# Decode cache values: from weighted rows summed by a selector matmul to cache values as TensorE's stationary operand

## The chip, the cores and the metric

The kernel runs on one core of a Trainium2 chip. The metric is device time in microseconds, from the first to the last instruction and what the launch adds around it; lower is better. The kernel before was run three times: 1863.29, 1864.06 and 1867.74 us, a median of 1864.06 us. One further execution was profiled; it took 1859.84 us, and its span, from the first to the last instruction that the profiler recorded, is 1858.1 us. All times "at" which something happens count from the start of that span.

## The reference, cut to what matters

The model is one layer of a hybrid decoder. A prompt of 1024 positions and eight decode rows (one new position each, with caches of up to 2048 past positions) go through the same weights. The mixer has three patterns of dilated sliding-window attention (g = 0, 1, 2; 8 heads of 64) and a state-space branch. Two places of it are touched here.

The prompt's three patterns are merged position by position, weighted by their softmax denominators:

```python
def merge_patterns(outs, lses):
    alpha = jax.nn.softmax(jnp.stack(lses, axis=0), axis=0)
    o = sum(alpha[g][..., None] * outs[g] for g in range(N_PATTERNS))
    return o.reshape(o.shape[:-2] + (ATTN_OUT,))
```

The decode rows read, for each pattern, 128 cached keys and values (every first, fourth or sixteenth position) and the new one, and merge in the same way:

```python
    o = jnp.einsum('bthk,btkhd->bthd', p, sel[:, :, :, 1].astype(jnp.float32)) / den
```

So the decode output of row b and head h is a sum over three patterns and 128 positions of a softmax weight times a value row of 64 numbers, and a small term for the new position. In float32 this is 8 rows x 3 patterns x 128 positions x 512 values.

## The kernel before

Everything is float32. A projection is computed as three matmuls per tile, in float32r, on a high part and a low part: weights are loaded (`wr`, L149), rounded by ScalarE (`wh`, L164), and VectorE makes the rest (`wl = wr - wh`, L165). TensorE then runs `g += xh.wh + xh.wl + xl.wh` over eight k tiles of 128 (`unit`, L176): 24 matmuls of 344 columns make one tile of 128 outputs by a third of the 1032 columns (1024 prompt positions and 8 decode rows). `wr`, `wh` and `wl` have two buffers each.

The stage in question lies between the attention of the last pattern and the output projection, from about 870 to 1040 us. Its work, all in flight together:

- **z projection** (L870 to L893): for k = 0 to 7 a weight load, three tiles of 24 matmuls (L176), a copy out of PSUM by ScalarE (`zt`, L877), SiLU, and VectorE's product with the state-space result (`yg`, L886).
- **Weights of the prompt's merge** (L818 to L848): softmax statistics are loaded (`sn`), a chain of small VectorE steps makes `wo`, TensorE transposes it (`wtp`, L845), ScalarE copies it (`wts`, L847), and it is stored to DRAM as `w_d` (L848).
- **The prompt's merge** (L849 to L862): 16 pieces (four column quarters by four head pairs). A piece loads the three patterns' outputs (`nt`, 128x768, L853) and the weights, broadcast to 64 partitions twice (`wt`, two loads, L856). GpSimd multiplies them (L858), VectorE adds the three thirds (L859, L860), ScalarE rounds the sum (`ah`, L861), and VectorE makes the rest (`al`, L862). `nt` and `wt` have two buffers, so the load of piece i+2 waits for piece i: `nt` until its L862 is done, `wt` until its L858 is. Below the pieces are called a to p, in pairs; their `nt` tiles are numbered 8474, 8484, 8494 and so on to 8624.
- **Decode values** (L895 to L924): for each decode row b, three value tiles are loaded (`cvt`, 128 positions x 512, L904, six buffers). Each is multiplied by its softmax weights `dpt`, broadcast along 64 columns (L907; pattern 0 on VectorE, 1 and 2 on GpSimd), VectorE adds the three (L910, L911), and one float32 matmul with a selector column sums over the positions into row b of a PSUM tile (L912, 512 moving columns). At the end ScalarE copies the eight rows out (L915), four transposes turn them (L918), and VectorE adds the new positions' terms (`dat`, L919 to L921).
- **Output projection, state-space part** (L930 to L976): VectorE and ScalarE split `yg` into `sh` and `sl` (L935, L936), and TensorE starts the first two output tiles together, m = 0 and m = 1 (L957), with two weight loads of its own (`wl` of m = 0 and m = 1, made on VectorE like the z weights). The tiles m = 2 to 7 follow through `unit`.

Each engine runs its instructions in one fixed order, and so does SyncE, which issues all these DMAs. A scheduler builds the orders beforehand from priorities ("evac" first, then "w", "side", "late", and "main" for the big matmuls) and its own estimate of durations; on the chip an instruction that waits holds all that stand behind it in its engine's order. `behind(ins, prev)` only fixes an order on one engine: each decode row's first matmul stands behind a chosen tile of the z projection (`zlast[CACHE[b]]`). `sel`, the selector, is set up by two memsets (L897, L898).

Of the kernel before, what the change touches and what calls it, by code (L numbers as in the profile page):

```python
# [8 lines left out]
F32 = mybir.dt.float32  # L9
# [7 lines left out]
P = 128  # L17
# [33 lines left out]
def trunk(tc, a, o):  # L51
# [67 lines left out]
    def behind(ins, prev):  # L119

        tc.add_manual_dep(ins.ins, prev.ins.name,
                          mybir.DependencyInfo(mybir.DependencyClass.NoSync, mybir.DependencyReason.DATA),
                          reason="order")
# [694 lines left out]
    with prio("late"):  # L818
# [30 lines left out]
        for q in range(S // QT):  # L849
            for hp in range(HP):  # L850
                qs = slice(q * QT, (q + 1) * QT)
                nt = mgp.tile([P, NG, QT], F32, tag="nt", name="nt")
                nc.sync.dma_start(out=nt, in_=n_d[:, hp, :, qs].rearrange("g p t -> p g t"))  # L853
                wt = mgp.tile([P, NG, QT], F32, tag="wt", name="wt")
                for h in range(2):
                    nc.sync.dma_start(out=wt[h * 64:(h + 1) * 64],  # L856
                                      in_=w_d[:, 2 * hp + h, qs].unsqueeze(0).to_broadcast([64, NG, QT]))
                nc.gpsimd.tensor_tensor(out=nt, in0=nt, in1=wt, op=ALU.mult)  # L858
                nc.vector.tensor_tensor(out=nt[:, 0], in0=nt[:, 0], in1=nt[:, 1], op=ALU.add)  # L859
                nc.vector.tensor_tensor(out=nt[:, 0], in0=nt[:, 0], in1=nt[:, 2], op=ALU.add)  # L860
                nc.scalar.copy(ah[:, hp, qs], nt[:, 0])  # L861
                nc.vector.tensor_tensor(out=al[:, hp, qs], in0=nt[:, 0], in1=ah[:, hp, qs], op=ALU.subtract)  # L862
# [30 lines left out]
                    nc.gpsimd.tensor_tensor(out=acc, in0=acc, in1=zt, op=ALU.add)  # L893

    with prio("late"):  # L895
        sel = cap.tile([P, NB * NB], F32, name="sel")
        nc.vector.memset(sel, 0.0)  # L897
        nc.vector.memset(sel[:, 0:NB * NB:NB + 1], 1.0)  # L898
        ops = att_ps("nps")
        for b in range(NB):  # L900
            vts = []
            for g in range(NG):
                vt = cvp.tile([P, 512], F32, tag="cv", name="cvt")
                nc.sync.dma_start(out=vt, in_=a[f"cache{g}"][b].rearrange("(k r) c -> r k c", r=DIL[g])[0, :, 512:1024])  # L904
                pw = dpt[:, g].rearrange("p h (x b) -> p b x h", b=NB)[:, b].unsqueeze(3)
                v4 = vt.rearrange("p (x h d) -> p x h d", x=HP, h=2)
                (nc.gpsimd if g else nc.vector).tensor_tensor(out=v4, in0=v4, in1=pw.to_broadcast([P, HP, 2, 64]),  # L907
                                                              op=ALU.mult)
                vts.append(vt)
            nc.vector.tensor_tensor(out=vts[0], in0=vts[0], in1=vts[1], op=ALU.add)  # L910
            nc.vector.tensor_tensor(out=vts[0], in0=vts[0], in1=vts[2], op=ALU.add)  # L911
            behind(nc.tensor.matmul(ops[:NB], sel[:, b * NB:(b + 1) * NB], vts[0], start=(b == 0), stop=(b == NB - 1)),  # L912
                   zlast[CACHE[b]])
        osb = cvp.tile([NB, 512], F32, tag="cv", name="osb")
        nc.scalar.copy(osb, ops[:NB])  # L915
        otp = att_ps("nps")
        for hp in range(HP):
            nc.tensor.transpose(otp[:, hp * NB:(hp + 1) * NB], osb[:, hp * P:(hp + 1) * P], ident[:NB, :NB])  # L918
        nc.vector.tensor_tensor(out=dat, in0=otp[:, 0:HP * NB], in1=dnv[:, 0], op=ALU.add)  # L919
        for g in range(1, NG):  # L920
            nc.vector.tensor_tensor(out=dat, in0=dat, in1=dnv[:, g], op=ALU.add)  # L921
        dv = dat.rearrange("p (h b) -> p h b", h=HP)
# [584 lines left out]
```

## Time and profile before

| what | value |
|---|---|
| median of three runs | 1864.06 us (1863.29 to 1867.74) |
| profiled execution, its own time | 1859.84 us |
| its span | 1858.1 us |
| TensorE busy | 1773.7 us (95%) |
| VectorE busy | 1143.8 us (62%) |
| ScalarE busy | 782.1 us (42%) |
| GpSimd busy | 320.4 us (17%) |
| mean granted TensorE clock | 0.982 of 2.4 GHz |

TensorE is busy nearly everywhere, and the other engines far less. A busy share is an average over the whole program, so it doesn't tell what one stage is worth. For that one looks at a stretch of time: how long TensorE sat idle in it, at which clock it ran (a stretch shows 1.00 at 2.4 GHz, 0.50 at 1.2 GHz, and a mean of the two when both were granted), and what ended each idle time. "Chain of waits" means the chain of work that ended last, followed back from the end: at each step what released it.

### The profile page before, as it was taken

The page shows a single profiled execution, that of the slowest core. Times are in us where ns is not written, and L with a number is a line of the kernel's source. Part 1 is how long each engine was busy: PE and PEld are TensorE (multiplying, and loading weights), DVE is VectorE, ACT ScalarE, POOL GpSimd, SP SyncE. Part 2 cuts the span into 40 slices and gives each one's busy share as a digit, 9 for nine tenths or more (in the row PEclk, how much of TensorE's full clock was granted, in tenths as well). Part 3 has the DMA queues.
Part 4 walks back from the last instruction along what each step waited for, and adds up shares of the span by engine and source line. Part 5 has one row for each costly group of instructions (what it writes and reads, how often), then busy time and mean ns, then how long its engine had stood idle before and what let it go on. Part 6 is the DMA issues. An engine that isn't in the chain of part 4 may idle for free.

```text
span 1858.1 us, 30703 instructions
## 1 busy us (share of the span) xinstructions
PE 1773.7 (95%) x12189; PEld 1659.7 (89%) x12189; DVE 1143.8 (62%) x2236; ACT 782.1 (42%) x1441; POOL 320.4 (17%) x217
## 2 busy tenths in 40 slices
PE   8999999999998999999879999999999999999995
PEld 6999877888887888988768999999999999999995
DVE  6545666776765454446577599886666666423338
ACT  5533554465544555556343335532222222431133
POOL 0000244544224221123342300000000000000020
PEclk9999999999999999999989999999999999999998
DMA  4322344434334243346566345364454445876686
GB/s 156 136 99 79 96 127 124 130 121 125 105 103 156 90 141 108 117 158 230 154 172 187 108 155 178 111 211 166 172 175 159 177 152 204 335 276 205 207 316 206
DMA packets 135200, 298.61 MB, mean 161 GB/s; under 512 B 18432, under 2 KB 85600, under 8 KB 133648
## 3 DMA queue, kind: packets, MB, share of 16 engines
q1 hardware_dynamic: 135056, 296.64, 48.2%
q8 instruction: 96, 1.57, 0.4%
q14 instruction: 48, 0.39, 0.1%
HBM read 247.49 MB, written 137.10 MB: 207 GB/s over the span
## 4 chain that ended last, share of the span: by engine, by line
PE 37%; DVE 8%; DMA 4%; issue 1%; ACT 1%; POOL 0%; SPq 0%; DVEq 0%; POOLq 0%; ACTq 0%
PE fb L1230 21%; PE g L176 15%; DMA nt<-n_d 2%; PE pg L176 1%; PE pu L176 1%; DVE wl L165 1%; DVE xr L1056 1%; DVE sl L936 1%; DVE nacc L1013 1%; DMA hr<-hid_d 0%; DMA cvt<-in_cache 0%; DVE nt L859 0%; POOL nt L858 0%; DMA wr<-in_w_fin 0%; DVE fl L1071 0%
## 5 line engine op out<-in xcount | busy, mean ns | idle before, releaser
L176 PE MATMUL g<-xh,wh 128*128 128x344 f32 x1344 | 445.0, 331 | 4.4 <-ACT rw L589 3.7
L176 PE MATMUL g<-xh,wl 128*128 128x344 f32 x1344 | 438.9, 327 | 7.2 <-DVE wl L165 7.2
L176 PE MATMUL g<-xl,wh 128*128 128x344 f32 x1344 | 440.6, 328 | 1.5 <-DVE xl L234 1.5
L176 PEld LDWEIGHTS g<-xh,wh 128*128 128x128 f32 x1344 | 256.5, 191 | 17.8 <-issue 8.4
L176 PEld LDWEIGHTS g<-xh,wl 128*128 128x128 f32 x1344 | 257.0, 191 | 15.0 <-DVE wl L165 8.0
L176 PEld LDWEIGHTS g<-xl,wh 128*128 128x128 f32 x1344 | 256.9, 191 | 7.8 <-issue 4.9
L1230 PE MATMUL fb<-fh,wsl 128*128 128x258 f32 x1216 | 222.3, 282 | 0.0
L1230 PEld LDWEIGHTS fb<-fh,wsl 128*128 128x128 f32 x1216 | 187.9, 189 | 0.0
L1230 PE MATMUL fb<-fl,wsl 128*128 128x258 f32 x608 | 171.7, 283 | 0.0
L165 DVE TENSOR_TENSOR wl<-wr,wh 128x1024 fp32r<-128x1024 f32 (+1 forms) x93 | 113.6, 1222 | 82.5 <-ACT wh L164 82.3
L176 PE MATMUL g<-hh,wh 128*128 128x344 f32 x432 | 137.9, 319 | 0.8 <-ACT fac L1297 0.8
L176 PE MATMUL g<-hh,wl 128*128 128x344 f32 x432 | 137.7, 319 | 0.0
L176 PE MATMUL g<-hl,wh 128*128 128x344 f32 x432 | 136.7, 320 | 0.0
L164 ACT CAST wh<-wr 128x1024 fp32r<-128x1024 f32 (+1 forms) x93 | 92.4, 995 | 93.5 <-PE g L176 87.8
L663 ACT ACTIVATE sm<-sm,ngm 128x128 f32<-128x128 f32 (+1 forms) x192 | 84.8, 443 | 108.9 <-DVE ngm L659 103.9
L1313 POOL TENSOR_TENSOR ow<-wr,ow 128x512 fp32r<-128x512 f32 x8 | 10.9, 1395 | 659.6 <-ACT ow L1312 659.6
L619 POOL TENSOR_TENSOR sw<-sw,sin 128x1032 f32<-128x1032 f32 x24 | 73.4, 3059 | 250.6 <-ACT sw L618 187.1
L1230 PEld LDWEIGHTS fb<-fl,wsl 128*128 128x128 f32 x608 | 114.8, 189 | 0.0
L618 ACT COPY sw<-rw 32x1032 f32<-32x1032 f32 x96 | 101.0, 1052 | 1.4
L589 ACT COPY rw<-g 128x344 f32<-128x344 f32 x108 | 47.2, 442 | 112.1 <-PE g L176 70.4
L1234 DVE TENSOR_TENSOR fo<-fp,fb 128x258 f32<-128x258 f32 x152 | 62.8, 420 | 46.1 <-PE fb L1230 43.7
L176 PEld LDWEIGHTS g<-hh,wh 128*128 128x128 f32 x432 | 81.1, 188 | 1.1 <-ACT fac L1297 1.1
(362 smaller groups left out, 3789.8 us busy)
## 6 DMA issues: line engine op xcount, KB each, us to landing
out_skv<-in_cache SPq DMA_DIRECT2D x64, 1023.5 KB, 5.8
wr<-in_w_in SPq DMA_DIRECT2D x56, 512.0 KB, 3.7
out_skv<-in_cache SPq DMA_DIRECT2D x16, 1022.0 KB, 5.5
wr<-in_w_out SPq DMA_DIRECT2D x24, 512.0 KB, 3.7
hr<-hid_d SPq DMA_DIRECT2D x22, 516.0 KB, 6.2
hid_d<-fo SPq DMA_DIRECT2D x38, 258.0 KB, 4.2
wg<-in_w_fin SPq DMA_DIRECT2D x19, 512.0 KB, 4.6
wu<-in_w_fin SPq DMA_DIRECT2D x19, 512.0 KB, 5.0
```

The costliest lines, as they stand in the source:

```text
L164: nc.scalar.copy(wh[:, :cols], wr[:, :cols])
L165: nc.vector.tensor_tensor(out=wl[:, :cols], in0=wr[:, :cols], in1=wh[:, :cols], op=ALU.subtract)
L176: last = nc.tensor.matmul(ps, x[:, ws], y[:, c0:c1], start=(k == 0 and j == 0), stop=(k == n - 1 and j == 2))
L589: return nc.scalar.copy(rw[:, c0:c1], ps)
L618: nc.scalar.copy(sw[q * 32:(q + 1) * 32, 0:T], rw[s * 32:(s + 1) * 32, :])
L619: nc.gpsimd.tensor_tensor(out=sw[:, 0:T], in0=sw[:, 0:T], in1=sin, op=ALU.mult)
L663: nc.scalar.activation(out=sm[:, h, :nk], in_=sm[:, h, :nk], func=AF.Exp, scale=SCALE, bias=ngm[:, g, j, i:i + 1], accum_out=den[:, g, j, ...
L936: nc.vector.scalar_tensor_tensor(out=lo, in0=yg[k][:, cs_], scalar=nw(SSD_NORM, k), in1=hi, op0=ALU.mult, op1=ALU.subtract)
L1013: nc.vector.tensor_tensor(out=acc, in0=acc, in1=sq, op=ALU.add)
L1056: nc.vector.scalar_tensor_tensor(out=h, in0=mv, scalar=nw(MIX_POST, m), in1=h, op0=ALU.mult, op1=ALU.add)
L1230: nc.tensor.matmul(ps, x[:, ks], y, start=(k == 0 and j == 0), stop=(k == 3 and j == 2))
L1234: return nc.vector.tensor_tensor(out=dst, in0=x, in1=y, op=ALU.add)
```

## The change

Three edits.

1. **Merge of the prompt.** The product of `nt` and `wt` (L858, 16 times) goes from GpSimd to VectorE.
2. **Decode values.** The 24 products, the 16 sums, the selector and its eight matmuls, the copy `osb` and the four transposes go. Instead each `cvt` tile goes to TensorE as it was loaded: for each decode row b and each head pair x, three float32 matmuls (one per pattern, summed in PSUM) take a 128x128 block of values as the stationary operand, and two columns of softmax weights move (one for each head of the pair). That is 8 x 4 x 3 = 96 matmuls of two moving columns. Each makes 128x2 results, of which one half of the partitions is used for either head.
3. **`dat`.** Two additions of 64 partitions each pick the halves out of PSUM (they were one addition of 128).

```diff
-                nc.gpsimd.tensor_tensor(out=nt, in0=nt, in1=wt, op=ALU.mult)
+                nc.vector.tensor_tensor(out=nt, in0=nt, in1=wt, op=ALU.mult)
...
-        sel = cap.tile([P, NB * NB], F32, name="sel")
-        nc.vector.memset(sel, 0.0)
-        nc.vector.memset(sel[:, 0:NB * NB:NB + 1], 1.0)
         ops = att_ps("nps")
...
-                pw = dpt[:, g].rearrange("p h (x b) -> p b x h", b=NB)[:, b].unsqueeze(3)
-                v4 = vt.rearrange("p (x h d) -> p x h d", x=HP, h=2)
-                (nc.gpsimd if g else nc.vector).tensor_tensor(out=v4, in0=v4, in1=pw.to_broadcast([P, HP, 2, 64]),
-                                                              op=ALU.mult)
                 vts.append(vt)
-            nc.vector.tensor_tensor(out=vts[0], in0=vts[0], in1=vts[1], op=ALU.add)
-            nc.vector.tensor_tensor(out=vts[0], in0=vts[0], in1=vts[2], op=ALU.add)
-            behind(nc.tensor.matmul(ops[:NB], sel[:, b * NB:(b + 1) * NB], vts[0], start=(b == 0), stop=(b == NB - 1)),
-                   zlast[CACHE[b]])
-        osb = cvp.tile([NB, 512], F32, tag="cv", name="osb")
-        nc.scalar.copy(osb, ops[:NB])
-        otp = att_ps("nps")
-        for hp in range(HP):
-            nc.tensor.transpose(otp[:, hp * NB:(hp + 1) * NB], osb[:, hp * P:(hp + 1) * P], ident[:NB, :NB])
-        nc.vector.tensor_tensor(out=dat, in0=otp[:, 0:HP * NB], in1=dnv[:, 0], op=ALU.add)
+
+            for x in range(HP):
+                q = x * NB + b
+                for g in range(NG):
+                    ins = nc.tensor.matmul(ops[:, 0:64].rearrange("p (h c) -> p h c", h=2)[:, :, q],
+                                           vts[g][:, x * P:(x + 1) * P], dpt[:, g, :, q], start=(g == 0),
+                                           stop=(g == NG - 1))
+                    if x == 0 and g == 0:
+                        behind(ins, zlast[CACHE[b]])
+        for h in range(2):
+            hs = slice(h * 64, (h + 1) * 64)
+            nc.vector.tensor_tensor(out=dat[hs], in0=ops[hs, h * 32:(h + 1) * 32], in1=dnv[hs, 0], op=ALU.add)
```

In the changed kernel the decode matmuls stand in line 907, their loads in line 901, and later lines are five lower than before (`sl` is L931, the two first output tiles L952).

With these edits the scheduler builds other orders. Three places are shown. In the rows a name's number tells one tile from another: `wl_9184` is the weight rest for z tile k = 6 in both kernels.

**VectorE ahead of the weights for z tile k = 6.** `nt_8474` and `nt_8484` are merge pieces a and b, `nt_8494` and `nt_8504` c and d; `yg4` is the product for k = 4. Before:

```order
L859 TENSOR_TENSOR nt_8474<-nt_8474 128x256
L860 TENSOR_TENSOR nt_8474<-nt_8474 128x256
L859 TENSOR_TENSOR nt_8484<-nt_8484 128x256
L165 TENSOR_TENSOR wl_9184<-wr_9182,wh_9183 128x1024
L862 TENSOR_TENSOR al_8436<-nt_8474,ah_8435 128x256
L860 TENSOR_TENSOR nt_8484<-nt_8484 128x256
```

After:

```order
L862 TENSOR_TENSOR al_8436<-nt_8484,ah_8435 128x256
L858 TENSOR_TENSOR nt_8494<-nt_8494,wt_8496 128x768
L859 TENSOR_TENSOR nt_8494<-nt_8494 128x256
L860 TENSOR_TENSOR nt_8494<-nt_8494 128x256
L858 TENSOR_TENSOR nt_8504<-nt_8504,wt_8506 128x768
L862 TENSOR_TENSOR al_8436<-nt_8494,ah_8435 128x256
L859 TENSOR_TENSOR nt_8504<-nt_8504 128x256
L860 TENSOR_TENSOR nt_8504<-nt_8504 128x256
L862 TENSOR_TENSOR al_8436<-nt_8504,ah_8435 128x256
L165 TENSOR_TENSOR wl_9184<-wr_9182,wh_9183 128x1024
```

The weight rest stood in the midst of pieces a and b; now all of a to d stand ahead of it.

**VectorE ahead of the second weight rest of the output projection** (m = 1: `wl_9539` before, `wl_9578` after), where `sl` is made. Before, with pieces g and h (`nt_8534`, `nt_8544`):

```order
L936 SCALAR_TENSOR_TENSOR sl0_9476<-yg0_8721,par_92,sh0_9475 128x344
L859 TENSOR_TENSOR nt_8534<-nt_8534 128x256
L936 SCALAR_TENSOR_TENSOR sl1_9478<-yg1_8811,par_92,sh1_9477 128x688
L936 SCALAR_TENSOR_TENSOR sl1_9478<-yg1_8811,par_92,sh1_9477 128x344
L860 TENSOR_TENSOR nt_8534<-nt_8534 128x256
L936 SCALAR_TENSOR_TENSOR sl2_9480<-yg2_8902,par_92,sh2_9479 128x688
L859 TENSOR_TENSOR nt_8544<-nt_8544 128x256
L936 SCALAR_TENSOR_TENSOR sl2_9480<-yg2_8902,par_92,sh2_9479 128x344
L165 TENSOR_TENSOR wl_9539<-wr_9537,wh_9538 128x1024
```

After, with the last pieces, o and p (`nt_8614`, `nt_8624`):

```order
L860 TENSOR_TENSOR nt_8614<-nt_8614 128x256
L931 SCALAR_TENSOR_TENSOR sl0_9515<-yg0_8721,par_92,sh0_9514 128x688
L931 SCALAR_TENSOR_TENSOR sl0_9515<-yg0_8721,par_92,sh0_9514 128x344
L858 TENSOR_TENSOR nt_8624<-nt_8624,wt_8626 128x768
L862 TENSOR_TENSOR al_8436<-nt_8614,ah_8435 128x256
L931 SCALAR_TENSOR_TENSOR sl1_9517<-yg1_8811,par_92,sh1_9516 128x688
L931 SCALAR_TENSOR_TENSOR sl1_9517<-yg1_8811,par_92,sh1_9516 128x344
L859 TENSOR_TENSOR nt_8624<-nt_8624 128x256
L931 SCALAR_TENSOR_TENSOR sl2_9519<-yg2_8902,par_92,sh2_9518 128x688
L931 SCALAR_TENSOR_TENSOR sl2_9519<-yg2_8902,par_92,sh2_9518 128x344
L860 TENSOR_TENSOR nt_8624<-nt_8624 128x256
L165 TENSOR_TENSOR wl_9578<-wr_9576,wh_9577 128x1024
```

Before, eight of the 16 pieces are behind this weight rest; now none is.

**SyncE, where decode row 2 is loaded** in the changed kernel (`cvt_9398`, `cvt_9400`, `cvt_9402`; row 3 is `cvt_9416` and the next two). After:

```order
L901 DMA cvt_9398<-in_cache0 128x512
L856 DMA wt_8496<-w_d_340 64x3x256 x2
L856 DMA wt_8506<-w_d_340 64x3x256 x2
L853 DMA nt_8494<-n_d_339 128x3x256
L901 DMA cvt_9400<-in_cache1 128x512
L853 DMA nt_8504<-n_d_339 128x3x256
L901 DMA cvt_9402<-in_cache2 128x512
L901 DMA cvt_9416<-in_cache0 128x512
```

Before, at the loads of pieces c and d, rows 5 to 7 are loaded:

```order
L904 DMA cvt_9428<-in_cache1 128x512
L904 DMA cvt_9431<-in_cache2 128x512
L856 DMA wt_8496<-w_d_340 64x3x256 x2
L904 DMA cvt_9437<-in_cache0 128x512
L856 DMA wt_8506<-w_d_340 64x3x256 x2
L904 DMA cvt_9440<-in_cache1 128x512
L149 DMA wr_9531<-in_w_out 128x1024
L853 DMA nt_8494<-n_d_339 128x3x256
```

Before, rows 0 to 4 are loaded ahead of all merge loads but the first two; now only rows 0 and 1 are, and rows 2 to 7 stand between the merge's loads.

## Rows read from the trace of the kernel before

**Rows 1.** The page: span, and each engine's busy time with its share and instructions.

```profile
span 1858.1 us, 30703 instructions
PE 1773.7 (95%) x12189; PEld 1659.7 (89%) x12189; DVE 1143.8 (62%) x2236; ACT 782.1 (42%) x1441; POOL 320.4 (17%) x217
```

**Rows 2.** Stretches of time (start:end): TensorE's busy time, granted clock, DMA share, GB/s.

```profile
895.00:960.00 65.00, 55.90 (x285) 0.89 0.63 170
960.00:1000.00 40.00, 29.89 (x150) 0.87 0.57 168
1000.00:1045.00 45.00, 40.78 (x255) 1.00 0.56 152
```

**Rows 3.** TensorE's waits, 890 to 1000 us: us in total, times, longest.

```profile
PE g L176 <- DVE wl L165: 7.3, 3, 4.1
PE g L957 <- DVE sl L936: 5.2, 1, 5.2
PE nps L912 <- DVE cvt L911: 2.4, 1, 2.4
PE ptp L965 <- ACT rt L202: 1.8, 1, 1.8
PE g L957 <- ACT sh L935: 1.7, 1, 1.7
```

**Rows 4.** TensorE's waits, 1000 to 1045 us.

```profile
PE g L176 <- DVE wl L165: 4.2, 3, 2.2
```

**Rows 5.** The chain of waits, 895 to 960 us: start, us, what.

```profile
895.92 2.59 DMA cvt<-in_cache
898.52 1.23 DVE wl L165
...
899.79 10.35 PE g L176 x47
...
912.40 0.48 ACT wts L847
...
929.82 6.25 DMA nt<-n_d
```

**Rows 6.** Line 858: nanoseconds min/median/max, first and last start.

```profile
L858 POOL TENSOR_TENSOR nt<-nt,wt x16: 1803/1846/2826, 921.9 to 1026.2; 128x768 f32<-128x768 f32 x16
```

**Rows 7.** Line 907, VectorE's part.

```profile
L907 DVE TENSOR_TENSOR cvt<-cvt,dpt x8: 677/692/1548, 875.2 to 940.2; 128x512 f32<-128x512 f32 x8
```

**Rows 8.** VectorE in order of time, one merge piece and the weights of m = 1.

```profile
960.22 0.42 DVE L859 TENSOR_TENSOR nt<-nt 128x256 f32<-128x256 f32 x1 [2.57 <-POOL nt L858]
960.68 0.43 DVE L860 TENSOR_TENSOR nt<-nt 128x256 f32<-128x256 f32 x1
...
961.64 0.42 DVE L862 TENSOR_TENSOR al<-nt,ah 128x256 fp32r<-128x256 f32 x1 [0.19 <-ACT ah L861]
962.75 1.42 DVE L936 SCALAR_TENSOR_TENSOR sl<-yg,par,sh 128x688 fp32r<-128x688 f32 x2 [0.69 <-ACT sh L935]
...
973.40 1.21 DVE L165 TENSOR_TENSOR wl<-wr,wh 128x1024 fp32r<-128x1024 f32 x1
```

**Rows 9.** VectorE in order of time, 955.9 to 963 us: one `yg`.

```profile
956.10 1.23 DVE L886 TENSOR_TENSOR yg<-yg,zt 128x1032 f32<-128x1032 f32 x1
```

**Rows 10.** DMA issues by line: KB each, median us to landing; then line 853 by itself.

```profile
cvt<-in_cache SPq DMA_DIRECT2D x24, 256.0 KB, 4.0
nt<-n_d SPq DMA_DIRECT2D x16, 384.0 KB, 4.9
wt<-w_d SPq DMA_DIRECT2D x32, 192.0 KB, 5.0
...
DMA to landing us min/median/max: 3.5/4.9/9.0
```

**Rows 11.** TensorE in order of time: four selector passes, four transposes.

```profile
914.18 1.88 PE L912 MATMUL nps<-cvt,sel 128*8 128x512 f32 x4
...
974.79 0.41 PE L918 MATMUL nps<-ident,osb 8*128 8x8 f32 x4
```

## The prediction

> **What bounds the kernel now.** The page comes first: TensorE is busy for 95% of the span and no other engine for more than 62% [rows 1]. So a gain must come out of TensorE's idle time, its clock or its work, and a loss comes from whatever makes it wait longer. The change touches only 870 to 1040 us, so I next read the windows of that stage. TensorE is busy 55.9 of 65 us, then 29.9 of 40, at granted clocks of 0.89 and 0.87; after 1000 us it is busy 40.8 of 45 us at 1.00 [rows 2]. Third, the waits say who ended those idle times: from 890 to 1000 us the weight rests `wl` 7.3 us, `sl` 5.2 and `sh` 1.7 us, the decode sum 2.4 us [rows 3]; and after 1000 us again `wl`, 4.2 us [rows 4]. Nearly all end on VectorE: TensorE has no work of its own that is late, it waits for an engine that runs merge pieces, decode sums and weight rests in one fixed order. Fourth, the chain shows how: a `cvt` load, then a weight rest queued behind the decode sum that needed that load, then 47 matmuls; further on an `nt` load of 6.25 us is itself the chain [rows 5]. What sits ahead of a weight rest in VectorE's order is what the stage costs.
>
> **The change part by part.** *Removed.* VectorE loses 8 products and 16 sums of 128x512 at 0.69 us [rows 7], 16.6 us; GpSimd loses 16 products (L858) of 1.85 us [rows 6] and 16 of the decode products. Nothing waits for GpSimd afterwards. TensorE loses eight selector matmuls (16 passes, four in 1.88 us, so 7.5 us) and four transposes of 0.10 us [rows 11].
>
> *Added to TensorE.* 96 float32 matmuls, 192 load-and-pass pairs if they split in two as the selector's do. No row shows such a pair with two moving columns. The four transposes, load and pass of eight columns, took 0.41 us together [rows 11], 0.10 each: 192 x 0.10 = 19.7 us. By the selector passes' 0.9 ns per column alone the passes would be nothing. I take 0.10, the nearer row, so net +12 us and between -8 and +12; if a full load each time is twice as dear, +32. What covers it comes below.
>
> *Added to VectorE.* 16 products of 128x768. A 128x256 operation takes 0.42 us [rows 8], 128x512 takes 0.69 [rows 7], 128x1024 takes 1.21 [rows 8]; 128x768 lies halfway between the last two, 0.95 us. 16 x 0.95 = 15.2 us against 16.6 removed, so VectorE's sum of work is unchanged. The order is not. Before, eight of the 16 pieces stood behind the weight rest of m = 1 (`wl_9539`); now all 16 stand ahead of its counterpart `wl_9578`, 12 ahead of m = 0's and four ahead of `wl_9184`, as the printed orders show. VectorE must therefore finish the whole merge before TensorE may begin the output projection in earnest, since there m = 0 and m = 1 alternate.
>
> *How long the merge takes.* `nt` has two buffers: the load of piece i+2 leaves when L862 of piece i is done, so loads and arithmetic alternate. I walk VectorE's order from the first L858 (time S) to the end of `wl_9578`, with 0.95 for L858, 0.45 for each addition and its gap, 0.42 for L862, 1.2 for a weight rest or `yg` [rows 8, 9], 1.42 for a pair of `sl`, and L from issue to landing of an `nt`:
>
> - a and b until c's load leaves (two products, four additions, one L862): 4.1
> - L; c, with d's product ahead of c's L862, until e's load leaves: 3.2
> - L; e and f as a and b: 4.1
> - L; g, with h's product and first addition, one weight rest and `yg5` ahead of g's L862: 6.1
> - L; i and j as a and b: 4.1
> - L; k as c: 3.2
> - L; m alone, then L; o's product, behind which n's L862 stands, which lets p's load go: 4.2 in all
> - L; p's product, o's L862, p's two additions, two pairs of `sl`, `wl_9578`: 6.3
>
> That is 35.3 us and eight landings in a row. The gaps in it, about twelve waits for ScalarE's `ah` at 0.19 us [rows 8], add 2.3: T = 37.7 + 8 L. For L there are the rows: median 4.9 us, shortest 3.5, longest 9.0 [rows 10]. I take the median: the pieces now come closer together, their loads (2 x 384 KB and 4 x 192 KB every 10 us or so, 157 GB/s) run beside the decode loads of 0.79 MB per row, and with the weights that is above the 170 GB/s of the busiest stretch [rows 2], so loads have no reason to get shorter. T = 37.7 + 39.2 = 76.9 us.
>
> *Where it starts.* Before, `wts` was copied at 912.40 us [rows 5] and the first L858 came at 921.9 [rows 6], 9.5 us later (store, weights' loads). In the changed kernel `wts` is earlier: the weight rest that ended at 899.75 stood behind a decode sum that waited for its load, TensorE's longest wait of 4.1 us [rows 3, 5]; and the 47 matmuls after it took 10.35 us, 0.22 each, where L176 at full clock takes about 0.157 (40.78 us busy over 255 matmuls is 0.160 in the stretch at 1.00 [rows 2]), so 7.5 us. Together 7 us: S = 912.4 - 7 + 9.5 = 914.9. The bounds are 912 and 922.
>
> *The end of it.* `wl_9578` ends at 914.9 + 76.9 = 991.8 us; `wl_9539` ended at 973.40 + 1.21 = 974.6 [rows 8]. TensorE has the same work behind either: +17.2 us. After it the merge is over, and the three waits of [rows 4] that weight rests behind late pieces caused are gone: -4.2. Net **+13.0 us**.
>
> *What hides TensorE's added work.* With wl_9184 behind piece d (4.1 + 3.2 + L + about 3, S + 15) TensorE still has z tiles k = 6 and 7, 144 matmuls (23 us), and six decode rows (14.8 us) ahead of the output projection: that ends near S + 57 with some waits for `cvt` loads. `sh0`, which stands on ScalarE behind piece n's rounding, comes near S + 64, `wl_9578` at S + 77. So the added pairs cost nothing. If a pair took 0.20 us, TensorE would be at S + 70, still ahead of `wl_9578`.
>
> One sentence of the Trainium skill speaks against my L. [Rows 10] show 384 KB landing in 3.5 to 9.0 us, never less. The Trainium skill, "DMA: Bandwidth & Descriptors", section "Anatomy of one DMA — SWDGE (gpsimd) path", fits a transfer at 2.0 us plus its bytes over 436 GB/s, an estimate of 2.9 us here (it was fitted on another queue's path): T would be 61 us and the net effect -3 us. The trace's shortest landing disagrees.
>
> **Rivals.** *(1) Short landings, no change that can be measured.* If decode rows no longer wait for GpSimd and VectorE, the queues may be calmer and L near its shortest. At L = 3.5, T = 65.7 and the net is 13.0 - 11.2 = +1.8 us. It breaks even at L = 3.3, and under L = 3.97 the loss is within 0.3%. For it: a landing of 3.5 us occurs. Against it: the median and the longest, 9.0 us [rows 10]. Time on the median's scale: 1866.
>
> *(2) Faster: the merge keeps ahead of TensorE.* If loads overlap the arithmetic more than my walk allows (two loads in flight, GpSimd no longer slowing VectorE, whose L907 went from 0.69 to 1.55 us at worst [rows 7]), the weight rests could come in time. Then the VectorE waits vanish, the `wl` 7.3, `sl` 5.2, `cvt` 2.4 and `wl` 4.2 us, 19.1 together; perhaps a few of them stay, and TensorE's +12 us stands uncovered, or +6 at half of it. Net -7 to -16, taken as -12: 1852. It needs T under about 57, L under 2.4, which no row shows.
>
> *(3) Slower still: TensorE or SyncE becomes last.* The loads of decode rows 2 to 7 now wait in SyncE's order for TensorE to free their buffers, ahead of `nt` and `wt` loads. Where a decode row is late, the merge's next load is late too. One such stop of a landing, 4 us by `cvt`'s median [rows 10], at two places, adds 8 us: 1885. It decides once a row's matmuls stand later on TensorE than the L862 that would have let the load go, which the walk above puts within a few us at row 5 (behind `wl_9184`).
>
> *(4) The pairs are dearer than all cover* (over 0.24 us each): TensorE ends its rows after `wl_9578`. No row is near that.
>
> **How the numbers follow.** The sum is on the profiled execution: 1859.84 + 13.0 = 1872.8. That execution is 4.2 us under the median of the runs, 1864.06; on the median's scale the forecast is 1864.06 + 13.0 = **1877**. 0.3% is 5.6 us, about what a measurement of this kernel can tell from no change. Chances: the forecast 0.60, rival 1 0.17, rival 2 0.13, rivals 3 and 4 0.10. Faster 0.13, the same 0.17, slower 0.70. For the range: the forecast's own unknowns are L (3.97 to 5.5, from -7.4 to +4.8) and S (-3 to +7), 1869 to 1888. To leave out no more than 2 in 10 it reaches over rival 1 down to 1858 and over most of rival 3 up to 1891.
>
> **What would show it right or wrong.** In the changed kernel's trace: the first L858 on VectorE near 915 us, each near 0.95 us; eight idle times of VectorE ended by `nt` or `wt` loads; the weight rest of m = 1 ending near 992 us, with a long wait of TensorE for `sh`, `sl` or `wl` just before; no waits of L176 for `wl` in the tiles that follow; decode matmuls at 0.10 us a pair or less. The prediction is wrong if `wl_9578` ends before 980, if landings are far from 4.9 us, if the chain runs over the decode matmuls instead of `nt` loads, or if the clock, which stood at 0.87 to 0.89 here, moves by as much as the waits do.

## The result, and the profile after

The changed kernel took 1882.62 us (median of four runs, 1881.81 to 1883.41) against 1864.59 us for the kernel before (four runs, 1863.29 to 1867.74). The ratio is 1.0106, with a 95% interval of 1.0085 to 1.0126: slower by 18 us, about 1%. The prediction was 1877 us, slower, with a range of 1858 to 1891.

The profiled execution took 1882.38 us. First the page: its span and the busy times of the engines, which answer to [rows 1].

```profile
span 1880.6 us, 30976 instructions
PE 1787.9 (95%) x12361; PEld 1681.9 (89%) x12361; DVE 1114.8 (59%) x2227; ACT 782.1 (42%) x1440; POOL 266.9 (14%) x185
```

VectorE and GpSimd do less than before, by 29 and 53.5 us, TensorE 14.2 us more, and the span is 22.5 us longer (more than the 18 us of the medians, since the profiled execution before was shorter than all four runs). So the summed work of TensorE explains part of the difference at most. The windows of the stage show where the rest is. Columns as in [rows 2]: TensorE busy, granted clock, DMA share, GB/s.

```profile
895.00:960.00 65.00, 58.25 (x357) 0.84 0.78 206
960.00:1000.00 40.00, 20.32 (x122) 0.71 0.58 159
1000.00:1045.00 45.00, 44.06 (x252) 0.96 0.27 90
```

From 960 to 1000 us TensorE is busy for half the time; before it was 29.89 of 40 us. Who ended its waits from 890 to 1000 us, as in [rows 3]:

```profile
PE g L952 <- ACT sh L930: 12.7, 1, 12.7
PE nps L907 <- DMA cvt<-in_cache: 9.0, 5, 5.9
PE g L952 <- DVE sl L931: 4.7, 2, 2.6
```

None of the waits for `wl` in [rows 3] is left, and after 1000 us one of 0.6 us is left of the 4.2 us in [rows 4]. In their place stand 17.4 us for `sh` and `sl` at the start of the output projection (L952), where it was 6.9 us before. Most of that is put down to ScalarE's `sh`, but ScalarE had nothing to do. Here is ScalarE in order of time (start, us, what; in brackets how long it was idle before, and for whom):

```profile
985.07 0.40 ACT L861 CAST ah<-nt 128x256 fp32r<-128x256 f32 x1 [6.09 <-DVE nt L860]
988.49 0.40 ACT L861 CAST ah<-nt 128x256 fp32r<-128x256 f32 x1 [3.02 <-DVE nt L860]
988.80 0.44 ACT L877 COPY zt<-g 128x344 f32<-128x344 f32 x1
989.14 1.34 ACT L930 ACTIVATE sh<-yg,par 128x688 fp32r<-128x688 f32 x2
```

`sh0` stands behind the rounding of merge piece n (L861 at 988.49), and that waits for VectorE's sum, which waits for a load. VectorE in order of time over pieces m to p shows it:

```profile
983.15 0.96 DVE L858 TENSOR_TENSOR nt<-nt,wt 128x768 f32<-128x768 f32 x1 [4.94 <-DMA nt<-n_d]
...
986.58 0.96 DVE L858 TENSOR_TENSOR nt<-nt,wt 128x768 f32<-128x768 f32 x1 [0.65 <-DMA nt<-n_d]
...
991.18 0.96 DVE L858 TENSOR_TENSOR nt<-nt,wt 128x768 f32<-128x768 f32 x1 [2.73 <-DMA nt<-n_d]
...
996.16 0.96 DVE L858 TENSOR_TENSOR nt<-nt,wt 128x768 f32<-128x768 f32 x1 [1.55 <-DMA nt<-n_d]
997.03 0.42 DVE L862 TENSOR_TENSOR al<-nt,ah 128x256 fp32r<-128x256 f32 x1
997.37 1.42 DVE L931 SCALAR_TENSOR_TENSOR sl<-yg,par,sh 128x688 fp32r<-128x688 f32 x2
...
1000.70 1.22 DVE L165 TENSOR_TENSOR wl<-wr,wh 128x1024 fp32r<-128x1024 f32 x1
```

The bracket of each product names an `nt` load. Over the whole stretch from 910 to 1005 us VectorE's waits are these, and the second row is the landing time of the `nt` loads (minimum, median, maximum):

```profile
DVE nt L858 <- DMA nt<-n_d: 35.6, 10, 6.3
```

```profile
DMA to landing us min/median/max: 3.5/6.2/8.3
```

Before, the median was 4.9 us [rows 10]. The chain of waits says the same in one list, from 951 us on, where it alternates between an `nt` load and a few VectorE instructions. Ahead of that it runs over TensorE's z and decode matmuls and one decode load:

```profile
918.17 7.50 DMA cvt<-in_cache
...
925.72 9.54 PE nps L907 x44
...
953.16 7.75 DMA nt<-n_d
...
965.49 6.05 DMA nt<-n_d
...
975.16 7.87 DMA nt<-n_d
...
985.96 4.75 DMA nt<-n_d
...
992.51 3.53 DMA nt<-n_d
```

### The profile page after: what moved, and what is told of

It reads as the page before. It is cut to its first block, busy times and chain, and to the rows that moved or that the text cites. A ratio compares the mean times of both kernels' runs of the same rounds, so it can differ in the third digit from the quotient of the medians.

```text
span 1880.6 us, 30976 instructions
## 1 busy us (share of the span) xinstructions
PE 1787.9 (95%) x12361; PEld 1681.9 (89%) x12361; DVE 1114.8 (59%) x2227; ACT 782.1 (42%) x1440; POOL 266.9 (14%) x185
## 4 chain that ended last, share of the span: by engine, by line
PE 73%; DMA 9%; DVE 8%; issue 4%; POOL 3%; ACT 3%; SPq 0%; DVEq 0%; POOLq 0%; ACTq 0%
PE g L176 39%; PE fb L1225 20%; PE pu L176 2%; DMA qb<-qd_d 2%; DMA nt<-n_d 2%; PE pg L176 2%; PE sps L649 2%; PE nps L683 1%; PE ptp L670 1%; POOL sw L619 1%; PE nps L907 1%; DMA hs<-in_ssm 1%; PE g L952 1%; ACT sw L618 1%; POOL kt L752 1%
## 5 line engine op out<-in xcount | busy, mean ns | idle before, releaser
L165 DVE TENSOR_TENSOR wl<-wr,wh 128x1024 fp32r<-128x1024 f32 (+1 forms) x93 | 109.1, 1175 | 90.2 <-ACT wh L164 90.1
```

The costliest lines, as they stand in the source:

```text
L165: nc.vector.tensor_tensor(out=wl[:, :cols], in0=wr[:, :cols], in1=wh[:, :cols], op=ALU.subtract)
```

## The experiments

Theory A was that of the prediction: merge pieces, with their loads one after another, stand ahead of `sh`, `sl` and the weight rests. Theory B: VectorE's 15 us of products are the loss, wherever they stand. Theory C: TensorE's decode matmuls and their loads are the loss. Each experiment is given with its ratio to the kernel before, run beside it on the same chip; that kernel's median was 1864.92 us beside the first four, 1868.80 us beside the first run with spread rows, the spread rows in the changed kernel, the two rows loaded and the kernel without decode values, 1865.24 us beside the second run with spread rows and the two with GpSimd, and 1866.63 us beside the one with three buffers. A median of one group can't be set beside that of another; the ratios can. Decode rows are counted from 1 here, so row 1 is the row b = 0 of the kernel.

**The merge's product alone**, in the kernel before:

```diff
-                nc.gpsimd.tensor_tensor(out=nt, in0=nt, in1=wt, op=ALU.mult)
+                nc.vector.tensor_tensor(out=nt, in0=nt, in1=wt, op=ALU.mult)
```

> The kernel before with only the merge's product (L858) moved to VectorE; the decode values stay as they were. VectorE has 8 pieces ahead of the weight rest of m = 1, as in the kernel before. Theory A (what counts is how many pieces stand ahead of the weight rests): within 6 us of before, 1859 to 1870. Theory B (VectorE's 15 us of products are the loss): 10 to 20 us slower, 1875 to 1885. Theory C (TensorE's new decode matmuls and their loads are the loss): as before, 1859 to 1870.

1865.15 us, ratio 1.0006 (0.9990 to 1.0021): no difference. Theory B falls; 16 products of 0.96 us on VectorE cost nothing where eight pieces stand ahead of the weight rest of m = 1.

**The decode matmuls alone**, the changed kernel with that line back on GpSimd:

```diff
-                nc.vector.tensor_tensor(out=nt, in0=nt, in1=wt, op=ALU.mult)
+                nc.gpsimd.tensor_tensor(out=nt, in0=nt, in1=wt, op=ALU.mult)
```

> The changed kernel with the merge's product back on GpSimd; the decode values on TensorE. The order that follows has 14 of 16 pieces ahead of the weight rest of m = 1 (16 in the changed kernel, 8 before), and each product takes 1.85 instead of 0.96 us. Theory A: as slow as the changed kernel or a little slower, 1878 to 1892, VectorE waiting for nt loads and for GpSimd. Theory B: as before, 1859 to 1870. Theory C: as the changed kernel, 1876 to 1885.

1884.59 us, ratio 1.0115 (1.0095 to 1.0135): the whole loss is there with this edit alone. TensorE's two longest waits from 890 to 1010 us, then VectorE's longest from 910 to 1005 us:

```profile
PE g L952 <- ACT sh L930: 9.2, 1, 9.2
PE nps L907 <- DMA cvt<-in_cache: 4.1, 4, 2.0
```

```profile
DVE nt L859 <- POOL nt L858: 46.7, 8, 10.9
```

This speaks for A or C. The edit that changes no merge piece is the one that moves them all: in the order built for it 14 pieces stand ahead of the weight rest of m = 1, against eight in the kernel before and in the first experiment. The next two tell A from C: they leave all the work of the change in place and only fix the order on VectorE.

**Half of the pieces behind the weight rest of m = 1**, in the changed kernel. `prods` collects the 16 products (L858), `rests` the weight rests (L165):

```diff
     ws = [ssm_w(m) for m in range(2)]
+    for i in range(8, 16):
+        behind(prods[i], rests[-1])
```

> The changed kernel with the products of pieces 9 to 16 fixed behind the weight rest of m = 1 on VectorE, so that 8 pieces stand ahead of it as in the kernel before; all else is the same work. Theory A: TensorE's waits for sh and sl (12.7 and 4.7 us) mostly go; TensorE is through its decode rows at 977 us and starts the output projection there, instead of 990; some 4 to 6 us come back as waits for weight rests among the late pieces: 1867 to 1874. Theory B and C: no gain beyond 3 us, 1879 to 1885.

1867.01 us, ratio 1.0017 (1.0004 to 1.0031). Of the 1.06% about 0.9 points are back. From 890 to 1000 us TensorE has one kind of wait left, and from 960 to 1000 us it is busy nearly throughout and at full clock:

```profile
PE nps L909 <- DMA cvt<-in_cache: 5.9, 2, 4.3
```

```profile
960.00:1000.00 40.00, 39.73 (x252) 1.00 0.42 130
```

**The old order throughout**, in the changed kernel. Pieces c and d go behind the weight rest of z tile k = 7, e to h behind that of m = 0, i to p behind that of m = 1:

```diff
     ws = [ssm_w(m) for m in range(2)]
+    for i in range(2, 16):
+        behind(prods[i], rests[-1 if i >= 8 else -2 if i >= 4 else -3])
```

> The changed kernel with VectorE's merge pieces fixed where they stood before: pieces 3 and 4 behind the weight rest of z tile k = 7, pieces 5 to 8 behind that of m = 0, pieces 9 to 16 behind that of m = 1. Theory A: the weight rests come first, TensorE is through its z tiles earlier; the decode loads, less mixed with merge loads, also land earlier: 1858 to 1868, at or below the kernel before. Theory C: TensorE still loses its waits for decode loads and its half-clock stretches: 1873 to 1885.

1866.15 us, ratio 1.0013 (0.9994 to 1.0031): as fast as the kernel before, within what was expected of A. C in its strong form falls. But the better order does not make it faster either, and the windows show what stands against it now: TensorE is busy 61.78 of 65 us, at a clock of 0.76.

```profile
895.00:960.00 65.00, 61.78 (x349) 0.76 0.60 167
```

The same kernel in finer stretches: from 907 us z matmuls, from 911.42 us rows 1 and 2 of the decode together (48 pairs of weight load and pass), then z matmuls; at 930 us rows 3 and 4.

```profile
907.00:911.40 4.40, 4.40 (x29) 1.00 0.14 29
911.40:917.00 5.60, 5.60 (x40) 0.72 0.65 102
917.00:922.50 5.50, 5.50 (x23) 0.50 0.70 186
930.00:939.00 9.00, 9.00 (x44) 0.50 0.45 160
```

The clock went from 1.00 (2.4 GHz) to 0.50 (1.2 GHz) while TensorE was busy without a gap, in the run of 48 pairs, and the z matmuls after it ran at half clock. Call it theory D: long runs of these matmuls cost the clock.

**Each decode row behind a z tile of its own**, with the old order, so that 24 pairs stand together at most:

```diff
-CACHE = ((4, 0), (4, 1), (4, 2), (5, 0), (5, 2), (6, 1), (7, 0), (7, 2))
+CACHE = ((4, 1), (4, 2), (5, 1), (5, 2), (6, 1), (6, 2), (7, 1), (7, 2))
```

> As the run with VectorE's pieces in their old order, and each decode row's 12 matmuls put behind a z tile of its own, so that no two rows stand together on TensorE (before: rows 1 and 2 together, then 3 and 4). In the run without this the granted clock was 0.76 from 895 to 960 us, at half from the first 24 matmuls in a row on. Theory D (long runs of two-column matmuls cost the clock): it stays above 0.9 there, 6 to 12 us gained, 1854 to 1861. Rival (the clock falls whatever the spacing, or the decode loads hold TensorE): 1863 to 1870.

1860.75 us over five runs, ratio 0.9947 (0.9931 to 0.9964). The time is as theory D had forecast, the clock is not: above 0.9 was expected, and the profile shows 0.84.

```profile
895.00:960.00 65.00, 62.53 (x380) 0.84 0.59 171
```

The profiled execution was the slowest of the five (1872.77 us), so I ran the same kernel again, beside others.

> The run with spread decode rows and the old order once more, beside the two others, for its clock and its gain on another set of runs. Theory D: the granted clock from 895 to 960 us above the 0.76 of the run without spreading, 1855 to 1862, faster than before by 0.3 to 0.6%. If the first gain was chance: 1863 to 1868.

1863.39 us over ten runs, ratio 0.9991 (0.9976 to 1.0006): the time that was expected if the first gain was chance. The two intervals do not overlap, so the gain over the kernel before is not settled: it lies between nothing and 0.7%. The second profile has the clock that theory D had forecast:

```profile
895.00:960.00 65.00, 62.15 (x420) 0.95 0.71 201
```

So one kernel shows 0.84 in one execution and 0.95 in another, and against the run before it the time is better by 0.7 points or by 0.2. A profile is a single execution, and these were not typical ones. The 0.76 comes from an execution with the lowest mean clock of that kernel's ten (0.976, where the mean of the ten is 0.980), the 0.95 from the one with the highest of its ten (0.983, where the mean is 0.980 too). Over all runs the spacing left the mean clock where it was (0.981 in the five runs above), so theory D is not shown.

**The same spacing with the order left to the scheduler**, that is the changed kernel with only that line:

> The changed kernel with the same spacing of the decode rows, and VectorE's order left to the scheduler: 14 pieces stand ahead of the weight rest of m = 1 (16 in the changed kernel). Theory A (the merge ahead of the weight rests is the loss): the clock is better but TensorE only waits longer, 1875 to 1884. Theory D as the main cause of the loss: 1862 to 1870.

1878.29 us, ratio 1.0047 (1.0029 to 1.0065). In time it is where A put it, slower than before, but it is also 0.6 points better than the changed kernel. The clock, which A and D both had better, is not: 0.83 from 895 to 960 us, against 0.84. Its order has 14 pieces and the product of a fifteenth ahead of the weight rest of m = 1 instead of 16, and two instead of four ahead of that of k = 6, so the run doesn't say how much of the gain is the spacing and how much the order. With the second experiment, which had 14 pieces ahead and the whole loss, it also says that the count of pieces alone does not set the price.

**Only two decode rows loaded**: rows 3 to 8 read the tiles of rows 1 and 2, so 18 of 24 value loads are left out and the output is not that of the reference.

```diff
+            if b > 1:
+                vts = kept[b % 2]
```

> The changed kernel in which decode rows 3 to 8 read the tiles of rows 1 and 2: 18 of the 24 value loads (4.7 MB) are left out, all matmuls stay. It asks why nt loads took 6.2 us here and 4.9 before. If the decode loads between them are the cause: median 4.5 to 5, the merge 8 x 1.2 to 1.7 us shorter, 1868 to 1873. If the merge's loads delay each other: median near 6, 1879 to 1885.

1882.44 us, ratio 1.0075 (1.0060 to 1.0090). By ratio a quarter to a third of the loss is gone, by the median nothing; by either the loss stays. TensorE waits for no decode load any more and is busy from 895 to 960 us without a gap, and all the time that it wins is waited away at the next place. The windows, TensorE's waits from 890 to 1000 us, and the landings of `nt`:

```profile
895.00:960.00 65.00, 65.00 (x397) 0.84 0.50 135
960.00:1000.00 40.00, 18.83 (x126) 0.73 0.60 170
```

```profile
PE g L957 <- ACT sh L935: 16.4, 1, 16.4
PE g L957 <- DVE sl L936: 4.8, 1, 4.8
```

```profile
DMA to landing us min/median/max: 3.8/5.8/8.0
```

So TensorE does not set the end of the stage here: freed of its waits for decode loads, it only waits longer for the merge. What the decode loads cost the merge this run doesn't price, since its order differs in a second way: TensorE transposes the merge's weights at 910.5 us instead of 902.5, so the first product comes at 919.7 instead of 911.4 us. From there to the end of the weight rest of m = 1 it took 85.3 us instead of 90.5; without the late start some 5 us would have been gained, as an estimate. The landings of `nt` stay long for the most part: 5.8 us without these loads, 6.2 with, 4.9 before.

**Three buffers for `nt`** (and five for the decode values in place of six, to fit), in the changed kernel:

```diff
     mgp = pool(rst, "mgp", 2, side="right")
+    ntp = pool(rst, "ntp", 3, side="right")
     QT = 256
-    cvp = pool(rst, "cvp", 6, side="right")
+    cvp = pool(rst, "cvp", 5, side="right")
...
-                nt = mgp.tile([P, NG, QT], F32, tag="nt", name="nt")
+                nt = ntp.tile([P, NG, QT], F32, tag="nt", name="nt")
```

> The changed kernel with three buffers for nt in place of two (and five for the decode values in place of six, to fit). The order still has all 16 pieces ahead of the weight rest of m = 1. If the landings of nt, one after another, are what makes the merge long (8 of them in 90 us): a load now leaves a piece earlier, the merge takes 65 to 78 us, TensorE's wait of 17 us for sh and sl shrinks to under 8, 1866 to 1875. If the merge is bound by its number of bytes or by the decode loads in SyncE's order: no gain beyond 3 us, 1879 to 1886.

1874.23 us, ratio 1.0044 (1.0029 to 1.0060): 0.6 points better, all 16 pieces still ahead of the weight rest of m = 1. TensorE's only waits from 890 to 1000 us, and the longest group of VectorE's from 910 to 1005 us:

```profile
PE nps L908 <- DMA cvt<-in_cache: 14.1, 8, 4.7
```

```profile
DVE nt L859 <- DMA wt<-w_d: 30.1, 13, 9.0
```

(In this kernel L859 is the product.) The 17.4 us for `sh` and `sl` are gone, for two reasons. The merge is faster: from the first product (916.4 us) to the end of the weight rest of m = 1 (998.2) it takes 81.7 us instead of 90.5, though 65 to 78 was expected, and `sh0` is started 10.5 us earlier. And TensorE is later: the decode loads, one buffer fewer, now hold it for 14.1 instead of 9.0 us, and it is through with all that stands ahead of the output projection at 987.0 instead of 977.3 us. So the alternation of load and arithmetic made a good part of the wait, not all of it; VectorE now waits for `wt`, which still has two buffers.

**Without the decode values**, in the old order: no value loads, no decode matmuls, `dat` holds only the terms of the new positions.

> VectorE's pieces in their old order, and the decode values left out altogether: no value loads, no decode matmuls; dat holds only the new positions' terms. It prices the decode part itself. If TensorE bounds the stage once the order is mended: 21 us of pairs, the half clock and 3 us of waits go, 1840 to 1852. If the merge bounds it in any order: 1860 to 1868.

1841.16 us, ratio 0.9860 (0.9842 to 0.9878). The merge does not bound the stage once the order is mended. The old order with the decode part is 1.0013, so matmuls and loads together cost about 1.5% or 28 us; with spaced rows it is 0.9 or 1.3%, by the two ratios above. The pairs alone are 192 x 0.108 = 20.7 us at full clock, so most of it is probably TensorE's work; a run with the matmuls and without the loads in this order was not made.

**The decode values on GpSimd**, the other way round: in the first experiment's kernel all 24 products and 16 sums go to GpSimd, and the selector matmuls stay. Then the same with the fixed order.

```diff
-                (nc.gpsimd if g else nc.vector).tensor_tensor(out=v4, in0=v4, in1=pw.to_broadcast([P, HP, 2, 64]),
-                                                              op=ALU.mult)
+                nc.gpsimd.tensor_tensor(out=v4, in0=v4, in1=pw.to_broadcast([P, HP, 2, 64]),
+                                                              op=ALU.mult)
...
-            nc.vector.tensor_tensor(out=vts[0], in0=vts[0], in1=vts[1], op=ALU.add)
-            nc.vector.tensor_tensor(out=vts[0], in0=vts[0], in1=vts[2], op=ALU.add)
+            nc.gpsimd.tensor_tensor(out=vts[0], in0=vts[0], in1=vts[1], op=ALU.add)
+            nc.gpsimd.tensor_tensor(out=vts[0], in0=vts[0], in1=vts[2], op=ALU.add)
```

> The other way round: the merge's product on VectorE as in the change, the decode values as before but all 24 products and 16 sums on GpSimd, one selector matmul per row. VectorE loses 16.6 us, and no weight rest stands behind a decode load any more; TensorE keeps its 7.5 us of selector passes in place of 20.7 us of pairs. The order leaves 10 pieces ahead of the weight rest of m = 1. Theory A: 1850 to 1860, the rest of the waits on sh and sl. If VectorE's work or GpSimd's speed bounds the stage: 1862 to 1872.

> The same, with VectorE's pieces fixed behind the weight rests as in the old-order run (2 ahead of z tile k = 7's, 4 ahead of m = 0's, 8 ahead of m = 1's). Leaving the decode values out in this order gave 1841; with 7.5 us of selector passes and a few waits for GpSimd: 1846 to 1856. If GpSimd's row sums come too late for TensorE: 1858 to 1870.

1867.36 us, ratio 1.0010 (0.9997 to 1.0023), and 1866.00 us, ratio 1.0006 (0.9991 to 1.0020). Both expectations of A missed by 7 us and more, and both times lie where they were expected if GpSimd (or, in the first, VectorE) bounds the stage. From 870 to 1000 us TensorE now waits for GpSimd and a little for everyone; the first rows of the first of the two:

```profile
PE nps L912 <- POOL cvt L911: 7.7, 3, 2.7
PE g L957 <- DVE sl L936: 3.8, 1, 3.8
PE wtp L845 <- issue: 2.5, 1, 2.5
```

The waits for weight rests behind decode sums went, and the decode sums themselves took their place. I have no kernel that does all the work and is clearly faster than the kernel before; the spaced rows in the old order come nearest.

## Why the prediction was right, and by how much it was off

**The mechanism held.** The prediction said that the merge, in front of `sh`, `sl` and the weight rest of m = 1, would end late because eight landings of `nt` follow one another. The chain of the changed kernel lists five of them, the fixed orders take nearly the whole loss away, and a third buffer takes about half of it. What it did not say is which edit does it: it treated the order as a result of both. The decode matmuls alone bring it, the product's move alone does not.

**The start of the merge, S.** Forecast 914.9, measured 911.4 us: 3.5 us early.

**The product.** Forecast 0.95 us, interpolated; measured 0.96 (median):

```profile
L858 DVE TENSOR_TENSOR nt<-nt,wt x16: 944/958/2851, 911.4 to 996.2; 128x768 f32<-128x768 f32 x16
```

**The landings, L.** This is the term that was mis-sized. Forecast 4.9 us, the median before. The loads of c, e, g, i, k, m, o and p took 4.8, 7.3, 5.9, 7.8, 6.1, 7.9, 4.8 and 3.5 us (the last five are the rows of the chain above, with 7.75 for i), together 48 instead of 39.2: 9 us more. The text had said that loads had "no reason to get shorter" and then took the middle of the old ones. Why they got longer is open. The median is 5.6 to 6.8 us in every kernel with these decode matmuls and 4.4 to 5.0 in every other. Pieces that come closer together can't be the whole reason, since the kernels in the old order have 5.6 to 6.5 us too; nor can the decode loads, since without 18 of 24 it is still 5.8; nor can the summed traffic, which was 135 GB/s in that run from 895 to 960 us and 170 before. By the estimate from the Trainium skill, "DMA: Bandwidth & Descriptors", section "Anatomy of one DMA — SWDGE (gpsimd) path", 2.9 us would have been it; no landing of `nt` in any of these traces was under 3.4 us.

**The rest of the walk.** From the first product to the end of the weight rest it took 1001.9 - 911.4 = 90.5 us; less 48 of landings leaves 42.5, forecast 37.7. The difference of 4.8 is in a wait for `wt` (1.35 us at b), one for the second load of a pair (1.48 us at d) and two instructions that took 2 us longer than usual (a product of 2.85 us, an L862 of 2.48 us), with small gains elsewhere. Both slow ones overlap the only two instructions that GpSimd ran between 905 and 1005 us (L893 at 933.62 and 952.53 us, 2.38 us each); no run tests whether that is the cause. Of the prediction's own sums, the step for m to o adds up to 3.6 us by its prices and not 4.2, the 1869 of the range leaves S out (with it, 1867), and the -16 of the second rival follows from none of its terms (-13 does). None of these bears on the result.

**What ends it.** Here a step was wrong, though the sum survived. The prediction took the weight rest of m = 1 as the gate of TensorE, "since there m = 0 and m = 1 alternate". They do not at the start: TensorE's order goes through `sh0`, `sl0`, `sh1`, `sl1` with m = 0 only, and `sl1` was the last thing that it waited for before 1000 us. TensorE in order of time, before and after:

```profile
971.04 0.94 PE L957 MATMUL g<-sl,wh 128*128 128x344 f32 x2 [5.25 <-DVE sl L936]
```

```profile
998.35 0.94 PE L952 MATMUL g<-sl,wh 128*128 128x344 f32 x2 [2.09 <-DVE sl L931]
```

The shift between these is 27.3 us. The weight rest ended 3.6 us after the first (974.6) and 3.6 us after the second (1001.9), so it moved by the same 27.3 us, and the sum came out as if it had been the gate. That is luck. Forecast for the shift: 17.2.

**The gain afterwards.** Forecast -4.2 us, waits behind late pieces. From 1000 to 1045 us 0.9 us of waits is left (0.6 for a weight rest, 0.3 for `mix`), so -3.3. Then 27.3 - 3.3 = 24.0 us, against 22.5 between the spans; I have not followed the 1.5 us.

**TensorE's added work.** Forecast 0.10 us a pair and no cost. Pairs come 0.108 us apart at full clock (24 in 2.48 us, first to last), which fits, and 0.214 at half clock. No cost is right for the changed kernel, where TensorE was through early and leaving out its 9 us of decode waits only made it wait longer. It is wrong in the old order, where the decode part costs 28 us, and the prediction left out that pairs run at half clock (44 of them in 9.54 us, in the chain above). It also named cover of "S + 57" for TensorE; it was through at 977.3 us, S + 66, and only 12.7 us ahead of `sh0`.

**The rivals.** Short landings: no, they were longer. The merge ahead of TensorE: no. TensorE or SyncE last: the event that this rival describes did happen, in small. From 900 to 1000 us SyncE waited 2.5 us in all for TensorE ahead of decode loads, and the load of piece i left at 953.1 us, 1.5 us after g's L862 had let it go. TensorE's own 9.0 us of waits for decode loads hid behind the merge. Pairs dearer than all cover: no, 0.108 to 0.214 us against 0.24.

**Its signs of being wrong.** The prediction named four. `wl_9578` did not end before 980 us. The landings are away from 4.9 us, by a quarter. The chain does run over decode matmuls, up to 951 us, and then over `nt` loads: of the stretch from 895 to 1010 us the loads make 26.0% and the decode matmuls 15.2%. And the clock moved, from 0.89 to 0.84 (895 to 960 us) and from 0.87 to 0.71 (960 to 1000, where TensorE is idle for half the time). So the signs were mixed; it is the fixed orders that decide for the merge.

## What to carry to other kernels

Where a scheduler lays out fixed orders, more work on one engine can reorder all the others: look at what now stands ahead of each short instruction that the bounding engine waits for, before pricing the work itself. Price a chain of loads through two buffers as landings in a row, and with a range for the landing that goes above the old median: here it rose by a quarter. A wait that is put down to one engine (`sh` on ScalarE) may begin three steps earlier, at a load; follow each engine back in order of time. And a clock read from one profile is that of one execution: compare it with the mean clock of the other runs before building on it.

## What the runs showed of the hardware that was not expected

A float32 matmul with a 128x128 stationary block and two moving columns ran as two pairs of load and pass, at 0.108 us a pair, so 96 of them take 20.7 us; the eight selector matmuls of 512 columns that they replace took 7.5 us [rows 11], 0.47 us for each of 16 passes (with eight stationary columns instead of 128). A pass with two columns instead of 512 thus cost a little under a quarter, and twelve times as many of them cost more.

The granted clock can fall while TensorE is busy by the profile without a gap. In the old order it went from 1.00 to 0.50 over a run of 48 such pairs (the finer stretches there). In the changed kernel it was 0.99 during the 48 pairs and 0.69 in the 24 z matmuls behind them; after a run of 24 pairs (940.8 to 943.4 us) it stayed at 1.00:

```profile
906.60:912.00 5.40, 5.40 (x50) 0.99 0.61 117
912.00:917.30 5.30, 5.30 (x25) 0.69 0.64 169
943.40:951.00 7.60, 7.60 (x50) 1.00 0.72 221
```

That a run of 24 pairs is safe does not follow. In the first run with spread rows the clock fell behind one (917.6 to 920.3 us), again without a gap:

```profile
917.50:920.30 2.80, 2.80 (x27) 1.00 0.71 112
920.30:925.50 5.20, 5.20 (x25) 0.67 0.48 130
```

What sets the clock in these stretches is open; spacing the rows is not shown to help.
